# Eight blocks of the first feed-forward computed for both token halves at once, each pair of weight blocks in seven block products instead of eight

## The chip, the cores and the metric

The kernel runs on one core of a Trainium2 chip. A core has a matrix engine (TensorE, PE in the profile, with its weight loads as PEld), a vector engine (VectorE, DVE), a scalar engine (ScalarE, ACT), a general engine (GpSimd, POOL) and a queue that issues transfers (SyncE, SP). Each engine takes its instructions strictly in the order in which the program lists them; semaphores make one wait for another. The metric is device time in microseconds (us), lower is better.

## What is computed

The reference is a two-layer trunk on 1024 tokens with 1024 channels, in float32. Layer 0 mixes tokens by a forgetting attention and a pooling mixer, layer 1 by an RWKV-7 recurrence, and each is followed by a gated feed-forward of width 2816:

```python
def _swiglu(h, w_gate, w_up, w_down):
    return (jax.nn.silu(h @ w_gate) * (h @ w_up)) @ w_down

for layer in range(DEPTH):                 # DEPTH = 2
    h = _rmsnorm(x, mix_norm[layer])
    y = fox_pool_mixer(h) if layer == 0 else rwkv7_time_mix(h)
    x = x + y
    x = x + _swiglu(_rmsnorm(x, ffn_norm[layer]), ffn_w_gate[layer], ffn_w_up[layer], ffn_w_down[layer])
```

The change concerns the feed-forward of layer 0.

## The kernel before

Activations lie transposed: channels on the 128 partitions, tokens along the free axis. The tokens are split in two halves of 512, so a half of an activation is 8 tiles of 128x512, one per 128 channels. Every float32 operand is split into a rounded high part and a remainder (`part`, lines 257 to 261, for activations: a ScalarE copy, line 259, and a VectorE subtraction, line 260; `load_part`, lines 140 to 153, for weights: a transfer, line 150, a copy, line 151, a subtraction, line 152), and one product of a 128x128 weight block with a 128x512 activation is three matmuls (`mm3`, lines 163 to 165).

The feed-forward (`ffn`, from line 683) goes through 22 blocks of 128 hidden columns. A block of one token half is 24 matmuls for the gate, 24 for the up projection, and later 24 for its share of the down projection: 72 matmuls. Its VectorE work is the remainders of six 128x512 weight tiles, the gating products (lines 726 and 732), the remainder of the result (line 260) and two of the eight additions into the residual (line 705).

The program runs the two token halves one after the other, because the first half has to reach the recurrence early:

- Half 0 of the first feed-forward runs by itself: four blocks (`GP`), then eighteen (`G1`), in groups of four and a last group of two. The matrix engine has nothing else to do in this stretch.
- `rw.dense(0, ...)` computes the projections of the recurrence for half 0.
- The recurrence of half 0 is two jobs, `rw.job(0, 0)` and `rw.job(1, 0)`, of eight heads each. A job has a **preparation** (lines 1007 to 1148: scans, decay factors, small matmuls at lines 1029, 1060, 1074 and 1085, the inverse of triangular blocks as a chain of VectorE steps at lines 1096 to 1120, and four groups of 64 tiny matmuls at lines 1130 and 1140, each followed by copies, line 121 on ScalarE and line 123 on VectorE) and a **chunk loop** (lines 1157 to 1192: eight dependent chunks, each a chain of small matmuls at lines 1165, 1171, 1177, 1188 and 1190 with copies between, lines 1167, 1173, 1179, 1183).
- Half 1 of the first feed-forward is a generator, `f1`, that serves as **filler**: its 22 blocks (1584 matmuls, named `fm` in the profile) are handed out between the steps of the two jobs. `weave` takes as many matmuls from the filler as the main stream yields, and the jobs yield what `rw.fr` says: seven numbers per token half, one for each kind of step. 96 matmuls of `f1` are issued ahead of the projections, what is left after the jobs is issued by `run(f1)`, and then the same things follow for half 1, with layer 1's feed-forward as filler.

A scheduler orders each engine's instructions when the program is built, by the order in which they were written and by when their operands should be ready; on the chip the order is fixed. Tile pools decide how many buffers each kind of tile has: five for split weights (`k.wbufs`), two for raw ones (`k.rawbufs`), four PSUM tiles for products (`k.mm`) in this stretch.

The norm ahead of the feed-forward of half 1 is `on[1]`: eight squares and sums, a matmul with a constant (line 307), a logarithm and an exponential (lines 309, 310, each with a table load on ScalarE here), then `make_h` (lines 675 to 680) scales the eight tiles and splits them. Before, this stands behind the four blocks of `GP`.

Of the kernel before, what the change touches and what calls it, by code (L numbers as in the profile page):

```python
# [9 lines left out]
F32 = mybir.dt.float32  # L10
F32R = mybir.dt.float32r
AF = mybir.ActivationFunctionType
ALU = mybir.AluOpType
# [3 lines left out]
P = 128  # L17
# [3 lines left out]
HN = 512  # L21
FF = 2816
NFB = FF // P
# [57 lines left out]
def rd(ap):  # L81
    return ap.bitcast(F32)
# [53 lines left out]
def load_w(k, ap, tag="w", w=512, bufs=None, pool=None):  # L136

    p, n = ap.shape
    return [load_part(k, ap[:, c:c + min(512, n)], p, min(512, n), tag, w, bufs, pool) for c in range(0, n, 512)]


def load_part(k, ap, p, n, tag="w", w=512, bufs=None, pool=None):
    hi, lo = ((pool or k.wp).tile([P, w], F32R, tag=tag + i, name=nm(k, tag + i), bufs=bufs or k.wbufs) for i in ("hi", "lo"))
    raw = k.wp.tile([P, 512], F32, tag="wraw", name=nm(k, "wraw"), bufs=k.rawbufs)
    dst = raw[0:p, 0:n]
    if len(ap.shape) == 3:
        dst = dst.rearrange("p (a b) -> p a b", b=ap.shape[2])
# [4 lines left out]
    k.nc.vector.tensor_tensor(lo[0:p, 0:n], raw[0:p, 0:n], rd(hi[0:p, 0:n]), ALU.subtract)  # L152
    return hi, lo


def mm3(k, out, pairs, first=True, last=True):

    nc = k.nc  # L160
    n = len(pairs)
    for i, ((wh, wl), (xh, xl)) in enumerate(pairs):
        nc.tensor.matmul(out, wh, xh, start=(first and i == 0), stop=False)  # L163
        nc.tensor.matmul(out, wh, xl, start=False, stop=False)  # L164
        nc.tensor.matmul(out, wl, xh, start=False, stop=(last and i == n - 1))  # L165
        yield 3


# [42 lines left out]
def ahead(fill, n):  # L211

    while n > 0:
        n -= next(fill)
# [41 lines left out]

def part(k, hl, raw):
    hi, lo = hl
    k.nc.scalar.copy(hi, raw)  # L259
    k.nc.vector.tensor_tensor(lo, raw, rd(hi), ALU.subtract)  # L260
    return hi, lo
# [412 lines left out]
def make_h(k, norm, gain, x, acc, out, rs=None):  # L674
    nc = k.nc
    rs = rs or norm.rstd()
    for kt in range(KT):
        t = norm.tile("hn")
        nc.vector.scalar_tensor_tensor(t, x[kt], cvec(k, gain, kt), rs, ALU.mult, ALU.mult)
        out[kt] = part(k, pair(k, *acc), t)  # L680


def ffn(k, ins, L, halves, H, X, acc, tp, groups, after=None, silu=True, fb0=0):
    nc = k.nc

    def project(w):
        o = {half: pmm(k) for half in halves}
        for c in range(2):
            for half in halves:
                yield from mm3(k, o[half], [(blk(w, kt), H[half][kt]) for kt in range(4 * c, 4 * c + 4)], c == 0, c == 1)  # L690
        return o

    def down(n, fb0, acts, last):
        per = max(1, 4 // n)
        cur = None
        for half, m in [(half, m) for half in halves for m in range(8)] if last else [(half, m) for m in range(8) for half in halves]:
            if cur != m // per:
                cur = m // per
                w = []
                for f in range(0, n, 4):  # L700
                    c = min(4, n - f)
                    w.append(load_part(k, ins[f"wd{L}"][per * cur:per * cur + per, :, fb0 + f:fb0 + f + c].rearrange("m p f c -> p m f c"), P, per * c * P))
            o = pmm(k)
            yield from mm3(k, o, [(blk(w, (m % per) * n + i), acts[fb0 + i, half]) for i in range(n)])
            nc.vector.tensor_tensor(X[half][m], o, X[half][m], ALU.add)  # L705
            if last:
                after(half, m)


    behind = iter(())  # L710
    for gi, n in enumerate(groups):
        acts, sgs = {}, {}
        for fb in range(fb0, fb0 + n):
            g = yield from project(load_w(k, ins[f"wg{L}"][fb]))
            for half in halves:
                sg = sgs[half] = tp.tile([P, HN], F32, tag="nt", name=nm(k, "sg"), bufs=k.ntbufs)
                if silu:
                    k.last_silu = nc.scalar.activation(sg, g[half], AF.Silu)
                elif silu is None and k.sigm:
                    k.last_sig = nc.scalar.activation(sg, g[half], AF.Sigmoid)  # L720
                    nc.vector.tensor_tensor(sg, g[half], sg, ALU.mult)
                else:
                    nc.scalar.activation(sg, g[half], AF.Exp, scale=-1.0)
                    nc.scalar.activation(sg, sg, AF.Ln, bias=1.0)
                    nc.scalar.activation(sg, sg, AF.Exp, scale=-1.0)
                    nc.vector.tensor_tensor(sg, g[half], sg, ALU.mult)  # L726
# [9 lines left out]
    yield from behind  # L736


EXP_M05 = 0.6065306597126334
# [496 lines left out]
def build(ctx, tc, ins, outs, dbg=None, stop=99):  # L1236
    nc = tc.nc
    k = K()
# [5 lines left out]
    H = [[None] * KT for _ in range(2)]  # L1244
    X = [[None] * KT for _ in range(2)]
    xT = ins["xT"]
    outT = outs["out"]
    rw = Rwkv(k, ins, dram)

    def pool(n, side="left"):  # L1250
        c = ExitStack()
        p = c.enter_context(tc.tile_pool(name=n, bufs=1, side=side, reuse_waits="tile"))
        return c, p

    def psum(n):
        c = ExitStack()
        p = c.enter_context(tc.tile_pool(name=n, bufs=1, space=PSUM))
        return c, p
# [11 lines left out]
    c_x0, x0 = pool("x0")  # L1270
# [7 lines left out]
    y, sp = {}, {}  # L1278
# [27 lines left out]
    c_m, mp = pool("m1", "right")  # L1306
    c_t, tp = pool("t1", "right")
# [13 lines left out]
    on = [Norm(k, tp) for _ in range(2)]  # L1321
# [13 lines left out]
    c_wl, wl = pool("wl")  # L1335
    c_u, u = pool("u")
    U, M = (u, "u", 40), (mp, "h1", 24)
    make_h(k, on[0], "ffn0", X[0], U, H[0], rs0)
    c_ps.close()
    c_pf, pf = psum("psf")  # L1340
    c_ps, k.ps = psum("ps1")
    k.mm = (k.ps, "mm", 4)

    norms = [Norm(k, tp), Norm(k, mp)]

# [9 lines left out]
            cover[half]()  # L1355
            rw.norm(half, norms[half].rstd(), XT[half])

    GP, G0, G1, G2 = ((4,),(),(4,4,4,4,2),(4,4,4,4,2))
    n = sum(GP) + sum(G0)
    g0 = ffn(k, ins, 0, (0,), H, X, U, tp, GP)  # L1360
# [5 lines left out]
    run(ffn(k, ins, 0, (0, 1), H, X, U, tp, G0, fb0=sum(GP)))  # L1366
    run(ffn(k, ins, 0, (0,), H, X, U, tp, G1, after0, True, n))
    rw.ln_exp, rw.mx, rw.wl_bufs, k.sigm = False, U, 2, True
    f1 = chain(ffn(k, ins, 0, (1,), H, X, M, mp, GP, silu=None), ffn(k, ins, 0, (1,), H, X, M, mp, G2, after0, None, n))
# [4 lines left out]
    for c in (c_u, c_wl, c_x0, c_t, c_ps):  # L1374
        c.close()
    c_ps, k.ps = psum("ps2")
    k.sbufs = 3
# [43 lines left out]
    c_t, tp = pool("tail0")  # L1421
# [129 lines left out]
```

## Time and profile before

| | |
|---|---|
| runs (3) | 2702.07 us median, 2700.6 to 2703.24 |
| the profiled execution's own time | 2699.79 us |
| its span | 2698.0 us |
| PE busy | 2632.5 us, 98% of the span, 15368 matmuls |
| DVE busy | 1725.1 us, 64%, 2940 instructions |
| ACT busy | 1298.7 us, 48%, 2297 instructions |
| chain of work that ended last | PE 77%, DVE 14%, ACT 3%, DMA 3%, issue 3% |

How to read it: the span is what the profiler saw between the first and the last instruction, 1.79 us less than the execution's own time. PE's busy time counts matmuls from start to end, and they overlap, so PE can read as 100% busy and still be held back for a moment. A row of a table of windows gives, for a stretch of the span in us, the stretch's length and then each engine's busy time with the number of instructions, the granted TensorE clock as a share of full speed, the share of time that the DMA engines moved data, and GB/s. A row of a timeline is the start, the duration, the engine, the line, the operation, the tiles written and read, and in brackets how long the engine sat idle before it and what ended that.

### The profile page before, as it was taken

How to read it: one execution, taken by the hardware profiler on the slowest of the kernel's cores; microseconds unless marked ns; L12 is line 12 of the kernel's file. 1: busy time of each engine (PE TensorE's matmuls, PEld its weight loads, DVE VectorE, ACT ScalarE, POOL GpSimd, SP SyncE). 2: the span in 40 equal slices, each digit the busy share in tenths (PEclk: the TensorE clock that was granted, in tenths of full speed). 3: DMA queues.
4: the chain of work that ended last, by engine and by line, in shares of the span. 5: the costliest groups of instructions: out<-in, count | busy, mean ns of one | idle time of the engine just before them, and what ended most of it. 6: DMA issues, size and time to landing. Idle time of an engine off the chain costs nothing.

```text
span 2698.0 us, 40269 instructions
## 1 busy us (share of the span) xinstructions
PE 2632.5 (98%) x15368; PEld 2072.6 (77%) x15368; DVE 1725.1 (64%) x2940; ACT 1298.7 (48%) x2297; POOL 49.4 (2%) x139
## 2 busy tenths in 40 slices
PE   8999999999999999999999999999999999999999
PEld 6787878788888777777777677777777777888887
DVE  8777684653446655975995676469778856534443
ACT  7555564443224766434634467664445444332232
POOL 1000000000001000000000000000000000000000
PEclk9999999999999999999999999999999999999999
DMA  4111131233333545424433534554244336333333
GB/s 136 58 51 57 42 98 48 83 96 98 96 96 113 172 161 189 129 83 131 148 91 99 195 94 160 168 179 128 87 138 140 92 97 202 101 98 96 97 97 94
DMA packets 170529, 306.11 MB, mean 113 GB/s; under 512 B 18896, under 2 KB 26192, under 8 KB 170336
## 3 DMA queue, kind: packets, MB, share of 16 engines
q1 hardware_dynamic: 156512, 278.38, 33.5%
q10 hardware_dynamic: 13824, 25.17, 2.5%
q8 instruction: 120, 1.97, 0.3%
q14 instruction: 73, 0.60, 0.1%
HBM read 257.04 MB, written 46.43 MB: 112 GB/s over the span
## 4 chain that ended last, share of the span: by engine, by line
PE 77%; DVE 14%; ACT 3%; DMA 3%; issue 3%; SPq 0%; DVEq 0%; ACTq 0%
PE mm L163 16%; PE mm L164 16%; PE mm L165 16%; PE fm L163 6%; PE fm L164 5%; PE fm L165 5%; DVE wlo L152 2%; PE mm L175 1%; DVE nu L1112 1%; DVE pd L1110 1%; DVE ZL L1068 1%; DMA wraw<-in_wd_dram 1%; DMA wraw<-in_wu_dram 1%; ACT whi L151 1%; PE o L1177 1%
## 5 line engine op out<-in xcount | busy, mean ns | idle before, releaser
L151 ACT CAST whi<-wraw 128x512 fp32r<-128x512 f32 x738 | 454.0, 617 | 886.8 <-PE mm L164 484.5
L152 DVE TENSOR_TENSOR wlo<-wraw,whi 128x512 fp32r<-128x512 f32 x738 | 501.3, 683 | 446.0 <-ACT whi L151 436.4
L163 PE MATMUL mm<-hh,whi 128*128 128x512 f32 x864 | 343.7, 400 | 6.7 <-ACT hh L355 6.2
L165 PE MATMUL mm<-hh,wlo 128*128 128x512 f32 x864 | 338.7, 392 | 0.0
L164 PE MATMUL mm<-hl,whi 128*128 128x512 f32 x864 | 337.8, 392 | 0.0
L163 PE MATMUL mm<-uh,whi 128*128 128x512 f32 x728 | 283.5, 391 | 0.9 <-DVE x L1318 0.9
L165 PE MATMUL mm<-uh,wlo 128*128 128x512 f32 x728 | 283.1, 389 | 1.2 <-DVE wlo L152 1.2
L164 PE MATMUL mm<-ul,whi 128*128 128x512 f32 x728 | 283.2, 390 | 0.0
L163 PE MATMUL fm<-h1h,whi 128*128 128x512 f32 x528 | 218.7, 415 | 14.8 <-DVE sg L726 10.6
L165 PE MATMUL fm<-h1h,wlo 128*128 128x512 f32 x528 | 208.7, 396 | 0.5 <-DVE wlo L152 0.5
L164 PE MATMUL fm<-h1l,whi 128*128 128x512 f32 x528 | 208.5, 395 | 0.1
L163 PEld LDWEIGHTS mm<-hh,whi 128*128 128x128 f32 x864 | 162.5, 188 | 43.1 <-ACT hh L355 6.9
L165 PEld LDWEIGHTS mm<-hh,wlo 128*128 128x128 f32 x864 | 162.7, 188 | 34.8 <-DVE wlo L152 0.6
L164 PEld LDWEIGHTS mm<-hl,whi 128*128 128x128 f32 x864 | 162.9, 189 | 32.7 <-DVE hl L260 1.3
L163 PE MATMUL fm<-hh,whi 128*128 128x512 f32 x416 | 172.4, 414 | 3.5 <-ACT hh L259 2.8
L164 PE MATMUL fm<-hl,whi 128*128 128x512 f32 x416 | 164.5, 396 | 0.2 <-DVE hl L260 0.2
L165 PE MATMUL fm<-hh,wlo 128*128 128x512 f32 x416 | 164.6, 396 | 0.0
L163 PEld LDWEIGHTS mm<-uh,whi 128*128 128x128 f32 x728 | 136.5, 188 | 34.6 <-issue 2.7
L164 PEld LDWEIGHTS mm<-ul,whi 128*128 128x128 f32 x728 | 136.6, 188 | 31.1 <-issue 1.1
L165 PEld LDWEIGHTS mm<-uh,wlo 128*128 128x128 f32 x728 | 136.7, 188 | 30.0 <-DVE wlo L152 2.0
L705 DVE TENSOR_TENSOR x<-mm,x 128x512 f32<-128x512 f32 x96 | 66.2, 692 | 119.8 <-PE mm L165 119.6
L163 PEld LDWEIGHTS fm<-h1h,whi 128*128 128x128 f32 x528 | 99.5, 189 | 48.7 <-DVE sg L726 13.3
(338 smaller groups left out, 4632.4 us busy)
## 6 DMA issues: line engine op xcount, KB each, us to landing
wraw<-in_wg_dram SPq DMA_DIRECT2D x176, 256.0 KB, 2.8
wraw<-in_wu_dram SPq DMA_DIRECT2D x176, 256.0 KB, 2.7
wraw<-in_wd_dram SPq DMA_DIRECT2D x176, 256.0 KB, 2.7
wraw<-in_w_in_dram SPq DMA_DIRECT2D x52, 256.0 KB, 2.9
x<-in_xT_dram SPq DMA_DIRECT2D x32, 256.0 KB, 4.8
x<-x SPq DMA_DIRECT2D x32, 256.0 KB, 3.1
wraw<-in_w_k_dram SPq DMA_DIRECT2D x32, 256.0 KB, 2.9
wraw<-in_w_v_dram SPq DMA_DIRECT2D x32, 256.0 KB, 3.0
```

Of the source, the lines that this page charges most:

```text
L151: k.nc.scalar.copy(hi[0:p, 0:n], raw[0:p, 0:n])
L152: k.nc.vector.tensor_tensor(lo[0:p, 0:n], raw[0:p, 0:n], rd(hi[0:p, 0:n]), ALU.subtract)
L163: nc.tensor.matmul(out, wh, xh, start=(first and i == 0), stop=False)
L164: nc.tensor.matmul(out, wh, xl, start=False, stop=False)
L165: nc.tensor.matmul(out, wl, xh, start=False, stop=(last and i == n - 1))
L175: k.nc.tensor.matmul(out[n * q:n * q + n], w[:, n * j:n * j + n], xs[j], start=c == 0, stop=c + g == len(xs), tile_position=(0, n * q))
L705: nc.vector.tensor_tensor(X[half][m], o, X[half][m], ALU.add)
L1068: nc.vector.tensor_tensor(ZL[h][HS[1 - h], i, bs], s4[HS[1]], self.msk[HS[1]].rearrange("p a t -> p (a t)").unsqueeze(1).broadcast_to([64, ...
L1110: nc.vector.tensor_tensor(pv, nu[:, j + 1:32, j:j + 1].broadcast_to([P, n, j]), nu[:, j:j + 1, 0:j].broadcast_to([P, n, j]), ALU.mult)
L1112: nc.vector.tensor_tensor(nu[:, j + 1:32, 0:j], nu[:, j + 1:32, 0:j], pv, ALU.add)
L1177: nc.tensor.matmul(sp[HS[h], i], BK[h][:, i, c], uv[h][:, i], start=True, stop=True)
```

## The change

For eight of the 22 blocks of layer 0's feed-forward, four pairs, gate and up are computed for both token halves together. A pair of weight blocks is a 2x2 arrangement (two halves of the channels by two blocks), the normed activations another (two halves of the tokens by two halves of the channels), and their product is done by Strassen's scheme in Winograd's form: seven products of 12 matmuls instead of eight, on sums and differences of the operands. `Joint.rows` builds the sums of the activations once, `Joint.four` builds those of the weights, runs the seven products and adds up their results, `Joint.down` does the down projection of a pair for both halves. Half 0's own run falls from 18 blocks behind `GP` to 10, and the filler `f1` from 22 to 14. `rw.fr` for half 0 is lowered, the products get six PSUM tiles instead of four, and the pool `wl` opens after the joint part, on the other side of the memory. Line numbers from 739 on are 148 higher in the changed kernel.

```diff
-def mm3(k, out, pairs, first=True, last=True):
+def mm3(k, out, pairs, first=True, last=True, again=False):
...
+class Joint:
...
+    def rows(self, gain, rs, H, U, M, keep):
...
+        for j in range(4):
+            a22 = normed(self.mt("a22"), 1, j + 4)
+            H[1][j + 4] = part(k, pair(k, *M), a22)
+            A["22"].append(H[1][j + 4])
+            a21 = normed(self.n3("a21"), 1, j)
+            nc.sync.dma_start(keep(j), a21)
+            s1 = self.nt("s1")
+            nc.vector.tensor_tensor(s1, a21, a22, ALU.add)
+            A["S1"].append(part(k, pair(k, *U), s1))
+            a11 = normed(self.jt("a11", "tt", 3), 0, j)
+            s2 = self.nt("s2")
+            nc.vector.tensor_tensor(s2, s1, a11, ALU.subtract)
+            A["S2"].append(part(k, pair(k, *U), s2))
+            nc.vector.tensor_tensor(a11, a11, a21, ALU.subtract)
+            A["S3"].append(part(k, pair(k, *M), a11))
+            a12 = normed(self.jt("a12", "tc", 2), 0, j + 4)
+            nc.vector.tensor_tensor(a12, a12, s2, ALU.subtract)
+            A["S4"].append(part(k, pair(k, *U), a12))
+            yield 0
...
+    def four(self, w, f, out):
...
+        p11 = self.split(b11)
+        t3, t2, t4 = (self.jt(n, "tt", 3) for n in ("t3", "t2", "t4"))
+        nc.vector.tensor_tensor(t3, b22, b12, ALU.subtract)
+        nc.vector.tensor_tensor(b12, b12, b11, ALU.subtract)
+        nc.vector.tensor_tensor(t2, b22, b12, ALU.subtract)
+        pt2 = self.split(t2)
+        x = pmm(k)
+        yield from product(x, p11, "11")
+        s1 = self.n3("p1")
+        nc.scalar.copy(s1, x)
+        p21 = self.split(b21)
+        nc.vector.tensor_tensor(t4, b21, t2, ALU.subtract)
+        y = pmm(k)
+        yield from product(y, pt2, "S2")
+        u = self.n3("u")
+        nc.vector.tensor_tensor(u, y, s1, ALU.add)
+        pt1 = self.split(b12)
+        yield from product(x, p21, "12", False)
+        out(0, 0, x, None)
...
+        yield from product(v, pt4, "22", False)
+        out(1, 0, v, u)
...
-    k.mm = (k.ps, "mm", 4)
+    k.mm = (k.ps, "mm", 6)
...
-    GP, G0, G1, G2 = ((4,),(),(4,4,4,4,2),(4,4,4,4,2))
...
+    GP, NJ = (4,), 4
+    left = NFB - sum(GP) - 2 * NJ
+    G1 = tuple(min(4, left - i) for i in range(0, left, 4))
+    fj, n = sum(GP), sum(GP) + 2 * NJ
+    g0 = ffn(k, ins, 0, (0,), H, X, M, tp, GP)
     ahead(g0, 24)
     for m in MO[1][NP:]:
         on[1].add(X[1][m])
-    run(g0)
-    make_h(k, on[1], "ffn0", X[1], M, H[1])
...
+    ahead(g0, 48)
+    jn = Joint(k, ins, 0, X, tp, mp, jp, M)
+    for _ in jn.rows("ffn0", (rs0, on[1].rstd()), H, U, M, lambda j: rw.dt(f"n{j}")):
+        ahead(g0, 24)
+    run(jn.run(fj, NJ, g0))
...
-    rw.fr = [6, 6, 5, 16, 7, 9, 16], [7, 7, 4, 16, 7, 8, 20]
+    rw.fr = [4, 4, 3, 8, 3, 9, 8], [7, 7, 4, 16, 7, 8, 20]
```

The order changes at two places that matter below. On VectorE, behind the sums of squares of half 1's norm, there stood only what the next blocks of half 0 need: remainders of weights (`wlo`), the gating product (`sg`) and the remainder of its result (`ul`).

```order
L732 TENSOR_TENSOR sg_4881<-mm_4895,sg_4881 128x512
L152 TENSOR_TENSOR wlo_4965<-wraw_4966,whi_4964 128x512
L152 TENSOR_TENSOR wlo_4971<-wraw_4972,whi_4970 128x512
L260 TENSOR_TENSOR ul_4922<-sg_4881,uh_4921 128x512
L152 TENSOR_TENSOR wlo_5007<-wraw_5008,whi_5006 128x512
```

At the same place of the changed kernel stand the rows of `Joint.rows` (lines 775 to 794, and 260 for their remainders). This is the end of the third of its four rounds; `wlo_5159` and `wlo_5165` are the weights of the next product of half 0, which TensorE runs before it comes to the joint part.

```order
L775 SCALAR_TENSOR_TENSOR a_1282_5149<-x_4538,cv,rs_4713 128x512
L789 TENSOR_TENSOR s_1277_5138<-s_1273_5130,a_1276_5136 128x512
L260 TENSOR_TENSOR ul_5133<-s_1273_5130,uh_5132 128x512
L791 TENSOR_TENSOR a_1276_5136<-a_1276_5136,a_1272_5126 128x512
L260 TENSOR_TENSOR ul_5141<-s_1277_5138,uh_5140 128x512
L794 TENSOR_TENSOR a_1282_5149<-a_1282_5149,s_1277_5138 128x512
L260 TENSOR_TENSOR h1l_5146<-a_1276_5136,h1h_5145 128x512
L152 TENSOR_TENSOR wlo_5159<-wraw_5160,whi_5158 128x512
L260 TENSOR_TENSOR ul_5153<-a_1282_5149,uh_5152 128x512
L152 TENSOR_TENSOR wlo_5165<-wraw_5166,whi_5164 128x512
```

So `wlo_5159` has moved behind 35 VectorE instructions that need half 1's norm, the first of them being the scaling of a tile by `rs_4964`; the next product's weights (`wlo_5237`) stand 17 rows further on.

On TensorE, near the end of the first job's preparation, filler matmuls (`fm`) stood between the groups of tiny matmuls (lines 1130 and 1140), of which these are the last two.

```order
L163 MATMUL fm_10826<-h1h_10293,whi_10820 128x512
L164 MATMUL fm_10826<-h1l_10294,whi_10820 128x512
L165 MATMUL fm_10826<-h1h_10293,wlo_10821 128x512
L163 MATMUL fm_10826<-h1h_10407,whi_10820 128x512
L164 MATMUL fm_10826<-h1l_10408,whi_10820 128x512
L165 MATMUL fm_10826<-h1h_10407,wlo_10821 128x512
L1140 MATMUL s_10833<-XR_9420,g_10796 32x32 x32
```

In the changed kernel (lines 1278 and 1288 are 1130 and 1140) nearly all of the filler of this part has gone.

```order
L1278 MATMUL s_11406<-t_2655_11375,XR_10428 32x32 x32
L165 MATMUL fm_11727<-h1h_7337,wlo_11716 128x512
L163 MATMUL fm_11727<-h1h_7343,whi_11715 128x512
L164 MATMUL fm_11727<-h1l_7344,whi_11715 128x512
L165 MATMUL fm_11727<-h1h_7343,wlo_11716 128x512
L1288 MATMUL s_11448<-XR_10428,g_11439 32x32
L1278 MATMUL s_11492<-t_2655_11375,XR_10428 32x32 x32
```

Counted in these orders, TensorE gets 403 filler matmuls in the first job's preparation before and 249 after, 432 and 269 in the second's; 168 and 76 in the first chunk loop, 168 and 72 in the second; 57 and 43 between the first loop and the second preparation. VectorE has 214 instructions in the first preparation before and 186 after, 224 and 191 in the second; of each number 144 or 146 are the job's own.

More of the change, by code (lines that the diff above doesn't have):

```diff
@@ L162, in mm3 @@
     for i, ((wh, wl), (xh, xl)) in enumerate(pairs):
-        nc.tensor.matmul(out, wh, xh, start=(first and i == 0), stop=False)
-        nc.tensor.matmul(out, wh, xl, start=False, stop=False)
-        nc.tensor.matmul(out, wl, xh, start=False, stop=(last and i == n - 1))
+        nc.tensor.matmul(out, wh, xh, start=(first and i == 0), stop=False, skip_group_check=again)
+        nc.tensor.matmul(out, wh, xl, start=False, stop=False, skip_group_check=again)
+        nc.tensor.matmul(out, wl, xh, start=False, stop=(last and i == n - 1), skip_group_check=again)
         yield 3
@@ L1334, in build @@
     c_h.close()
-    c_wl, wl = pool("wl")
     c_u, u = pool("u")
+    c_j, jp = pool("joint", "right")
     U, M = (u, "u", 40), (mp, "h1", 24)
@@ L1356, in after0 @@
             rw.norm(half, norms[half].rstd(), XT[half])
-    GP, G0, G1, G2 = ((4,),(),(4,4,4,4,2),(4,4,4,4,2))
-    n = sum(GP) + sum(G0)
-    g0 = ffn(k, ins, 0, (0,), H, X, U, tp, GP)
+    GP, NJ = (4,), 4
[3 more added lines that the diff above has]
+    g0 = ffn(k, ins, 0, (0,), H, X, M, tp, GP)
     ahead(g0, 24)
@@ L1363, in build @@
         on[1].add(X[1][m])
-    run(g0)
-    make_h(k, on[1], "ffn0", X[1], M, H[1])
-    run(ffn(k, ins, 0, (0, 1), H, X, U, tp, G0, fb0=sum(GP)))
+    ahead(g0, 48)
[3 more added lines that the diff above has]
+    run(jn.run(fj, NJ, g0))
+    for j in range(4):
+        t = jn.n3("a21")
+        nc.sync.dma_start(t, rw.dt(f"n{j}"))
+        H[1][j] = part(k, pair(k, *M), t)
+    c_j.close()
+    c_wl, wl = pool("wl", "right")
     run(ffn(k, ins, 0, (0,), H, X, U, tp, G1, after0, True, n))
     rw.ln_exp, rw.mx, rw.wl_bufs, k.sigm = False, U, 2, True
-    f1 = chain(ffn(k, ins, 0, (1,), H, X, M, mp, GP, silu=None), ffn(k, ins, 0, (1,), H, X, M, mp, G2, after0, None, n))
+    f1 = chain(ffn(k, ins, 0, (1,), H, X, M, mp, GP, silu=None), ffn(k, ins, 0, (1,), H, X, M, mp, G1, after0, None, n))
     f1 = using(k, f1, mm=(pf, "fm", 2), ntbufs=3)
@@ L1373, in build @@
     weave(rw.dense(0, XT[0], wl, tp), (f1, share))
-    for c in (c_u, c_wl, c_x0, c_t, c_ps):
+    for c in (c_u, c_x0, c_wl, c_t, c_ps):
         c.close()
```

74 lines of the change are left out of this document (added).

## The prediction

> **What bounds the kernel now.** The page first: TensorE is busy nearly all the time, so an idle engine elsewhere is worth nothing, and the question is how fast matmuls follow each other and where they don't. The table of windows answers both.
>
> ```profile
> span 2698.0 us, 40269 instructions
> ...
> PE 2632.5 (98%) x15368; PEld 2072.6 (77%) x15368; DVE 1725.1 (64%) x2940; ACT 1298.7 (48%) x2297; POOL 49.4 (2%) x139
> ...
> core 0: us, PE busy (x) PEld busy (x) DVE busy (x) ACT busy (x) POOL busy (x), PEclk, DMA share, GB/s
> ...
> 600.00:700.00 100.00, 100.00 (x443) 82.81 (x442) 41.66 (x63) 28.62 (x47) 0.00 (x0) 1.00 0.33 98
> 1050.00:1187.00 137.00, 126.83 (x970) 98.54 (x969) 125.28 (x212) 71.64 (x129) 4.44 (x15) 0.99 0.40 125
> 1187.00:1258.00 71.00, 71.00 (x855) 54.36 (x851) 38.29 (x73) 28.73 (x61) 0.25 (x1) 1.00 0.32 101
> 1258.00:1267.00 9.00, 9.00 (x43) 5.30 (x38) 2.94 (x6) 6.26 (x11) 0.74 (x2) 1.00 0.21 60
> 1267.00:1405.00 138.00, 129.73 (x852) 99.72 (x852) 131.56 (x222) 68.55 (x122) 4.20 (x16) 0.99 0.43 133
> 1405.00:1477.00 72.00, 72.00 (x923) 55.48 (x916) 39.39 (x72) 34.14 (x69) 0.00 (x0) 1.00 0.33 99
> 1477.00:1520.00 43.00, 41.34 (x236) 28.87 (x232) 27.25 (x46) 16.27 (x30) 0.00 (x0) 1.00 0.50 161
> ```
>
> 600 to 700 us is half 0's feed-forward alone: 443 matmuls in 100 us, 0.2257 us from one to the next, and VectorE 42% busy. This stretch is bound by TensorE and nothing else. 1050 to 1477 us are the two jobs of half 0: preparation, chunk loop, a short end, preparation, chunk loop. In the preparations **VectorE is busy 91% and 95%** (125.28 of 137, 131.56 of 138) and TensorE 93% and 94%: two engines are full at once. In the chunk loops TensorE is full and VectorE at 54%. So a matmul taken from the first stretch or from a chunk loop is worth its 0.2257 us; one taken from a preparation is worth only what VectorE loses with it. The list of waits confirms who is late there: its longest row for TensorE in the first preparation is a wait for VectorE.
>
> ```profile
> PE fm L163 <- DVE sg L726: 5.7, 3, 4.1
> ```
>
> **The change part by part.** *Matmuls.* Each gate or up of a pair takes 84 matmuls instead of 96; eight of them save 96, in all 96 x 0.2257 = 21.7 us. The mean duration of a matmul is no measure of that:
>
> ```profile
> L165 PE MATMUL mm<-uh,wlo 128*128 128x512 f32 x728 | 283.1, 389 | 1.2 <-DVE wlo L152 1.2
> ```
>
> 389 ns each would make it 37.3 us, but they overlap. The Trainium skill ("TensorE: Matmul & The Clock Gate", section "Wait — 56ns, not 53.3ns?") gives 215.7 ns from start to start at 512 columns; by it the saving would be an estimated 20.7 us. The trace's 225.7 ns decides.
>
> The 96 are a difference of two large moves. Half 0's run goes from 18 blocks (18 x 72 = 1296 matmuls) to four pairs of 264 and ten blocks of 72 (1776): 480 more, +108.3 us, all in a stretch where TensorE is alone. The filler loses eight blocks, 576 matmuls, 130.0 us. The orders show from where: 154 from the first preparation, 163 from the second, 188 from the chunk loops, 14 between, and the other 57 after the jobs.
>
> *Preparations.* 154 and 163 matmuls are 34.8 and 36.8 us of TensorE. VectorE loses 28 and 33 instructions, nearly all of 128x512. One of those costs this much in a row of them:
>
> ```profile
> 498.70 0.69 DVE L302 TENSOR_TENSOR sq<-sq,sq 128x512 f32<-128x512 f32 x1
> 499.30 0.68 DVE L260 TENSOR_TENSOR ul<-hn,uh 128x512 fp32r<-128x512 f32 x1
> 499.90 0.69 DVE L302 TENSOR_TENSOR sq<-sq,sq 128x512 f32<-128x512 f32 x1
> ```
>
> 0.60 us from start to start. So the preparations get shorter by 28 x 0.60 = 16.8 and 33 x 0.60 = 19.8 us, and 18.0 + 17.0 = 35.0 us of the matmuls taken out turn into idle TensorE. After the change TensorE's own work in the first preparation is 126.83 - 403 x 0.2257 = 36 us plus 249 x 0.2257 = 56 us, 92 us, against a VectorE floor of 125.28 - 16.8 = 108.5 us: the cover is gone, and VectorE alone is late. Bounds: if VectorE gets to 100% busy, the preparations last 108.5 and 131.56 - 19.8 = 111.8 us, and 16.9 us are lost; if the copies between the tiny matmuls, which have lost their filler, add 3 us to each, 41. I take 35, since VectorE's share was 91 to 95% with the filler there.
>
> *Chunk loops.* Here is a chunk without its filler: the matmuls of line 1165, the copy that waits for them, line 1171, its copies, then line 1177 and its two steps.
>
> ```profile
> 1191.06 0.69 PE L1165 MATMUL s<-SV,ZL 128*64 128x64 f32 x16
> ...
> 1191.79 0.42 DVE L1167 COPY zs<-s 128x256 f32<-128x256 f32 x1 [1.37 <-PE s L1165]
> ...
> 1193.26 0.68 PE L1171 MATMUL s<-zs,XR 64*64 64x64 f32 x16
> ...
> 1193.99 0.76 ACT L1173 COPY uv<-s 64x256 f32<-64x256 f32 x2 [0.93 <-PE s L1171]
> ...
> 1213.32 0.69 PE L1177 MATMUL o<-uv,BK 128*64 128x64 f32 x16
> ...
> 1214.05 0.42 DVE L1179 TENSOR_TENSOR st<-o,S 128x256 f32<-128x256 f32 x1 [0.71 <-PE o L1177]
> ...
> 1214.51 0.87 DVE L1183 TENSOR_TENSOR SV<-st,Pc 64x256 f32<-64x256 f32 x2
> ```
>
> From line 1165 to its copy's end 1.15 us, from line 1171 to its copies' end 1.49, from line 1177 to the new state 2.06: 4.7 us a chunk if nothing is in the way. A chunk lasts 71 / 8 = 8.9 us now and loses 92 / 8 = 11.5 matmuls, 2.6 us, to 6.3. The chain still fits, with 1.6 us to spare, but three matmuls (0.7 us) behind line 1171 no longer cover its copies, and a 0.6 us split ahead on ScalarE or VectorE then stalls TensorE. I take 0.4 us a chunk, 16 chunks, 6 us; bounds 2 and 14 (nothing but the bare chain; a split ahead at half of the three hand-overs).
>
> *Entry to the joint part.* `Joint.rows` adds 13 VectorE instructions in each of four rounds and needs half 1's norm. The norm comes after 72 matmuls that begin here:
>
> ```profile
> 492.62 0.70 PE L163 MATMUL mm<-uh,whi 128*128 128x512 f32 x2 [0.88 <-DVE x L1318]
> ```
>
> so at 492.6 + 72 x 0.2257 = 508.9 us. From that matmul to the first scaled tile the same norm took, later in the kernel before,
>
> ```profile
> 558.42 1.02 PE L307 MATMUL mm<-sq,cc 128*128 128x512 f32 x2
> ...
> 562.98 2.08 DVE L679 SCALAR_TENSOR_TENSOR hn<-x,cv,rs 128x512 f32<-128x512 f32 x3 [3.08 <-ACT rs L310]
> ```
>
> 4.6 us, with both table loads; one more split on ScalarE makes it 5.1. So the rows begin at about 514.0, and `wlo_5159`, 35 instructions behind the first, is ready at 514.0 + 36 x 0.61 = 536.0 (0.60, and a little more for the scalings, 0.66 us apart by the row above). TensorE has two products of 24 that need none of it, to 508.9 + 1.0 + 48 x 0.2257 = 520.7, and then waits about 15 us. The 24 end at 541.4; `wlo_5237` comes 17 rows later, at 546.4, another 5 us. After that the joint products' own weights are ready in time. Together **20 us**. In the kernel before, the norm waited behind `GP` and cost TensorE nothing. Bounds: 17 (0.55 us an instruction, 8% closer than these rows) and 24 (0.3 for each of ten waits on ScalarE besides). What hides none of this is VectorE's later slack: its order is fixed.
>
> *Inside the joint part* a pair is 264 matmuls, 59.6 us; VectorE has some 60 instructions for it, 37 us, and the order puts each product's weights at least one product (2.7 us) ahead. I take 3 us for the one place where products of `down` follow the last of `four` directly (add, product, split: about 2.7 us by these durations); bounds 0 and 12 (0.2 us at each of 56 products). Fewer weight transfers and splits are under TensorE anyway: nothing. The 57 + 14 matmuls elsewhere lie in windows with TensorE full: counted in the 21.7.
>
> **Sum:** -21.7 + 35.0 + 6 + 20 + 3 = +42.3 us. Against the profiled execution's own 2699.79 that is 2742; the median of the runs shown is 2.3 us above that execution (0.08%), well inside the bounds. Low ends together -21.7 + 16.9 + 2 + 17 + 0 = +14 (2714), high ends -21.7 + 41 + 14 + 24 + 12 = +69 (2769).
>
> **Rivals.** *VectorE is not the bound (faster).* If its instructions could stand closer, both the idle preparations and the entry's wait would go: 2699.8 - 21.7 + 9 = 2687. It would decide if 186 instructions fitted under TensorE's 92 us, 0.49 us each. For it speaks only that TensorE is as full as VectorE now; against it, that the mean of a busy preparation is 131.56 / 222 = 0.59 us with 5% idle. *A cold TensorE (slower still).* The preparations' rows grant a clock of 0.99 where the longest wait is 4.1 us, and 1.00 elsewhere. Waits of 15 us at the entry and repeated ones in the preparations could run their small matmuls, some 36 us in each, partly at a lower clock; a third of them at half speed is 12 us each on the way to VectorE: 2766. The Trainium skill ("TensorE: Matmul & The Clock Gate", section "What's actually happening") says that one idle window of about 3.4 us halves the clock until about 3.4 us of work have passed; the 0.99 agrees in sign. *Joint products stall at each hand-over (slower still).* A sum that arrives late at each of 56 products by 0.6 us is 34 us: 2773. Against it: five split buffers, and the products' weights stand ahead of the additions in the order. *The change doesn't save matmuls:* excluded by the orders, which hold 96 fewer.
>
> **How the numbers follow.** Forecast with its bounds, 2714 to 2769: 74%. VectorE not the bound: 7%. Both stalls at half, about 2706: 4%. Cold TensorE: 8%, half of it inside the forecast's bounds. Joint stalls: 7%. For the range I leave out the first rival and most of the last: 2707 to 2772. A difference of 0.2% is what a measurement of this kernel can tell from none; below 2696.7 lies most of the first rival, 6%; between that and 2707.5 5%; above 89%.
>
> **What would show it.** Right: a TensorE wait of 10 us or more for a `wlo` of line 152 around 520 us; preparations of 115 to 123 us with VectorE over 88% busy and TensorE under 82%; chunk loops of 52 to 56 us; half 0's feed-forward about 130 us later at its end. Wrong: preparations near 100 us, or no long wait at the entry. The sum fails if the chunk loops lose their cover altogether, or if the joint products wait for their sums.

## The result, and the profile after

The changed kernel takes **2736.42 us** (median of 4 runs, 2734.26 to 2741.7) against 2702.6 us (4 runs, 2700.6 to 2703.24): ratio **1.0129, 95% interval 1.0112 to 1.0147**, slower by 34 us. Its profiled execution took 2734.26 us. The page of the changed kernel begins:

```profile
span 2732.5 us, 40037 instructions
...
PE 2636.0 (96%) x15272; PEld 2075.3 (76%) x15272; DVE 1791.5 (66%) x3052; ACT 1287.5 (47%) x2281; POOL 50.2 (2%) x139
```

There are 96 matmuls fewer, and yet TensorE is busy 3.5 us longer: some matmuls have become slower. The table of windows shows where. The first row of each kernel runs from the start of the norm's 72 matmuls (492.6 us) to the first scan of the first job; then come preparation, chunk loop (first to last copy `zs`), the stretch between the jobs, preparation, chunk loop, and all the rest. Before:

```profile
492.60:1051.18 558.58, 557.38 (x2435) 449.67 (x2436) 286.19 (x441) 260.09 (x435) 11.73 (x22) 1.00 0.40 124
1051.18:1191.79 140.61, 130.44 (x1016) 101.35 (x1015) 126.77 (x215) 72.19 (x129) 4.44 (x15) 0.99 0.39 121
1191.79:1252.54 60.75, 60.75 (x717) 46.39 (x718) 33.06 (x64) 25.02 (x55) 0.00 (x0) 1.00 0.32 100
1252.54:1275.25 22.71, 22.71 (x140) 14.58 (x139) 13.11 (x23) 11.77 (x21) 1.11 (x3) 1.00 0.41 126
1275.25:1420.14 144.89, 136.62 (x1047) 106.79 (x1046) 133.73 (x225) 72.05 (x128) 4.09 (x15) 0.99 0.41 126
1420.14:1480.56 60.42, 60.42 (x716) 46.00 (x717) 32.16 (x63) 28.01 (x59) 0.00 (x0) 1.00 0.32 98
1480.56:2698.00 1217.44, 1186.10 (x7065) 928.78 (x7065) 746.95 (x1211) 547.18 (x959) 11.36 (x38) 0.99 0.40 126
```

After:

```profile
492.60:1182.27 689.67, 670.57 (x2919) 542.47 (x2920) 412.56 (x642) 298.13 (x499) 12.15 (x22) 0.99 0.33 104
1182.27:1298.05 115.78, 102.35 (x861) 79.81 (x860) 108.56 (x186) 56.63 (x104) 3.95 (x15) 0.88 0.36 115
1298.05:1342.79 44.74, 44.74 (x632) 32.55 (x631) 26.98 (x55) 21.20 (x48) 0.00 (x0) 0.96 0.36 113
1342.79:1364.64 21.85, 21.31 (x131) 12.81 (x131) 12.23 (x22) 9.81 (x18) 1.18 (x3) 1.00 0.29 83
1364.64:1484.44 119.80, 105.06 (x875) 80.92 (x876) 111.86 (x193) 58.98 (x106) 4.17 (x15) 0.92 0.39 120
1484.44:1527.11 42.67, 42.67 (x626) 30.86 (x624) 26.78 (x55) 17.96 (x43) 0.00 (x0) 0.99 0.37 119
1527.11:2732.50 1205.39, 1171.33 (x6996) 916.99 (x6996) 739.24 (x1200) 542.09 (x950) 12.10 (x38) 0.99 0.40 125
```

What a stage lost is its change in time, less 0.2257 us for each matmul more or fewer in it (the counts in brackets behind PE):

| stage | time before, after (us) | matmuls, at 0.2257 | lost |
|---|---|---|---|
| to the first scan | 558.58, 689.67 | +484: +109.2 | 21.9 |
| preparation 1 | 140.61, 115.78 | -155: -35.0 | 10.2 |
| chunk loop 1 | 60.75, 44.74 | -85: -19.2 | 3.2 |
| between | 22.71, 21.85 | -9: -2.0 | 1.2 |
| preparation 2 | 144.89, 119.80 | -172: -38.8 | 13.7 |
| chunk loop 2 | 60.42, 42.67 | -90: -20.3 | 2.6 |
| the rest | 1217.44, 1205.39 | -69: -15.6 | 3.5 |
| sum | +34.5 | -96: -21.7 | 56.3 |

So 56 us were lost against 21.7 saved. The first loss stands in the list of TensorE's waits (what waits, for whom, us in all, times, longest) as one row, and in the timeline as two matmuls:

```profile
PE mm L165 <- DVE wlo L152: 17.4, 2, 15.4
...
537.62 0.80 PE L165 MATMUL mm<-uh,wlo 128*128 128x512 f32 x1 [15.44 <-DVE wlo L152]
538.22 0.63 PE L163 MATMUL mm<-uh,whi 128*128 128x512 f32 x1
538.64 0.63 PE L164 MATMUL mm<-ul,whi 128*128 128x512 f32 x1
...
548.10 0.50 PE L165 MATMUL mm<-uh,wlo 128*128 128x512 f32 x1 [1.97 <-DVE wlo L152]
```

The two waits are `wlo_5159` and `wlo_5237` of the order. Between them stand 24 matmuls that take 548.10 - 537.62 - 1.97 = 8.5 us instead of 24 x 0.2257 = 5.4: behind the long wait they are 0.43 us apart. Entry: 15.4 + 2.0 + 3.1 = 20.5 us. Those 3.1 us cost nothing of their own: the second weights come when VectorE has made them, and faster matmuls would only have waited longer for them. From 600 to 1100 us TensorE is 99.8% busy, and of the stage's 21.9 us only 1.4 are left for everything but the entry; so the joint products hardly stall.

### The profile page after: what moved, and what is told of

Its sections match the earlier page's. It is cut to its first block, busy times and chain, and to the rows that moved or that the text cites. A ratio compares the mean times of both kernels' runs of the same rounds, so it can differ in the third digit from the quotient of the medians.

```text
span 2732.5 us, 40037 instructions
## 1 busy us (share of the span) xinstructions
PE 2636.0 (96%) x15272; PEld 2075.3 (76%) x15272; DVE 1791.5 (66%) x3052; ACT 1287.5 (47%) x2281; POOL 50.2 (2%) x139
## 3 DMA queue, kind: packets, MB, share of 16 engines
q8 instruction: 120, 1.97, 0.3%
## 4 chain that ended last, share of the span: by engine, by line
PE 75%; DVE 14%; DMA 4%; ACT 4%; issue 2%; SPq 0%; ACTq 0%; DVEq 0%
PE mm L163 17%; PE mm L164 17%; PE mm L165 17%; PE fm L163 5%; PE fm L165 4%; PE fm L164 4%; DVE wlo L152 2%; PE mm L175 1%; DVE ZL L1216 1%; PE s L1313 1%; ACT whi L151 1%; DMA wraw<-in_wg_dram 1%; PE o L1325 1%; DVE nu L1260 1%; PE s L1319 1%
## 5 line engine op out<-in xcount | busy, mean ns | idle before, releaser
L151 ACT CAST whi<-wraw 128x512 fp32r<-128x512 f32 x658 | 404.3, 616 | 774.8 <-PE mm L164 444.3
L152 DVE TENSOR_TENSOR wlo<-wraw,whi 128x512 fp32r<-128x512 f32 x658 | 446.9, 683 | 389.6 <-ACT whi L151 382.2
L165 PE MATMUL mm<-uh,wlo 128*128 128x512 f32 x664 | 259.6, 392 | 17.5 <-DVE wlo L152 17.4
L163 PE MATMUL mm<-uh,whi 128*128 128x512 f32 x664 | 259.6, 393 | 1.2 <-DVE x L1466 1.2
L164 PE MATMUL mm<-ul,whi 128*128 128x512 f32 x664 | 259.1, 391 | 0.0
L165 PEld LDWEIGHTS mm<-uh,wlo 128*128 128x128 f32 x664 | 125.3, 189 | 44.6 <-DVE wlo L152 18.8
L163 PE MATMUL fm<-h1h,whi 128*128 128x512 f32 x336 | 141.4, 421 | 8.5 <-DVE x L705 5.9
L165 PE MATMUL fm<-h1h,wlo 128*128 128x512 f32 x336 | 140.3, 418 | 1.4 <-DVE wlo L152 1.4
L164 PE MATMUL fm<-h1l,whi 128*128 128x512 f32 x336 | 139.0, 414 | 0.1
L163 PEld LDWEIGHTS fm<-hh,whi 128*128 128x128 f32 x416 | 79.1, 190 | 31.1 <-issue 8.1
```

The source lines that it names most:

```text
L164: nc.tensor.matmul(out, wh, xl, start=False, stop=False, skip_group_check=again)
```

## The experiments

**Is it the filler?** *The kernel before, with the changed `rw.fr`, without the joint part.*

```diff
-    rw.fr = [6, 6, 5, 16, 7, 9, 16], [7, 7, 4, 16, 7, 8, 20]
+    rw.fr = [4, 4, 3, 8, 3, 9, 8], [7, 7, 4, 16, 7, 8, 20]
```

> The kernel before with nothing changed but the seven numbers of rw.fr for half 0, which are set as in the changed kernel: the two jobs get the thin filler, the rest of the filler is issued after them; no joint part. Theory A (the loss of the two jobs comes from taking filler out of them, as the stages of the two traces add up: preparations 23.2 us, chunk loops 7.1, the stretch between and the one after 2.9): 2702.6 + 33 = 2736 us, between 2730 and 2742. By the prices of the prediction (35 + 6) it would be 2744. Rival B (the loss belongs to the joint part, its memory or its clock): 2703 us.

2740.01 us, ratio 1.0141 (1.0128 to 1.0154): 38 us lost with not one matmul fewer. By the same reckoning preparation 1 loses 10.6 us (10.2 in the changed kernel), preparation 2 16.2, the loops 3.3 and 3.7. The losses of the jobs need no joint part; rival B falls. (The time stands between theory A's 2736 and the 2744 by the prediction's prices.)

*Only the preparations' six numbers lowered* (`[4, 4, 3, 8, 7, 9, 8]`):

> The kernel before with rw.fr of half 0 lowered only for the preparations (six of the seven numbers, the fifth stays 7). Theory A: 23 to 24 us of loss, 2727 us (2721 to 2732), each preparation some 25 us shorter but with some 155 to 170 matmuls fewer. By the prediction's price 2738. Rival B (TensorE alone bounds the preparations, so that filler goes in and out at its own price): 2703 us.

*Only the chunk loops' number lowered* (`[6, 6, 5, 16, 3, 9, 16]`):

> The kernel before with rw.fr of half 0 lowered only for the chunk loops (the fifth number 7 becomes 3). Theory A (the chain of a chunk is no longer covered at some hand-overs): 7 us of loss, 2710 us (2707 to 2714), chunks of some 6.1 to 6.4 us instead of 8.6. Rival B (the loops stay bound by TensorE): 2703 us.

2718.13 us, 1.0067 (1.0055 to 1.0079), and 2712.98 us, 1.0038 (1.0025 to 1.0052). The first run is a miss: it cost less than theory A said, although the scheduler took 75 matmuls out of its loops too; its two preparations lost 9.1 and 7.7 us. The second run came out in its range but lost its time elsewhere than expected: its loops got shorter by 18.2 and 19.1 us for 84 matmuls (19.0) each, so they lost under 1 us together, while preparation 2 and the rest, whose numbers were not touched, lost 5.5 each, which stays open. Nor do the two add up to the first run: 1.05% against 1.41%. By the stages of the profiled executions, 3 us of the difference lie in preparation 2 (with the loops left full it kept more of its filler, 916 matmuls against 871), 3 in chunk loop 2 and 2 behind the jobs.

**Is it VectorE?** The prediction called VectorE full in the preparations. *The filler's weights that are loaded during the jobs get no remainder* (the third matmul of a product takes the rounded weights once more), in both kernels:

```diff
     k.nc.scalar.copy(hi[0:p, 0:n], raw[0:p, 0:n])
+    if getattr(k, "nolo", False):
+        return hi, hi
```

> The changed kernel, in which the filler's weights that are loaded during the two jobs of half 0 get no remainder (load_part returns the rounded part twice): 20 and 23 VectorE subtractions fewer in the two preparations, 7 or 8 fewer in each chunk loop, the same matmuls. Theory A (VectorE's count of instructions sets the length of the thinned preparations): 20 x 0.60 = 12.0 and 23 x 0.60 = 13.8 us shorter at most, preparations of 103 to 107 us instead of 116 and 120, 2736.4 - 24 = 2712 us (2704 to 2718). Rival B (the job's own chain through ScalarE, VectorE and TensorE sets it): preparations within 4 us of the changed kernel's, 2728 us or more.

> The kernel before with the same edit: 36 and 39 VectorE subtractions fewer in the two preparations, the same matmuls. Theory A (before the change VectorE and TensorE are both full there, so VectorE relieved by more than 20 us leaves TensorE as the bound): each preparation 8 to 10 us shorter, near 131 and 137 us, 2702 - 17 = 2685 us (2680 to 2691). Rival B (the preparation's idle TensorE comes from the job's own chain): 2697 us or more.

Before: 2700.05 us, 1.0004 (0.9995 to 1.0013). Nothing, where theory A wanted 17 us. The two preparations of that run:

```profile
1053.72:1191.34 137.62, 129.72 (x1014) 102.42 (x1013) 107.28 (x179) 71.03 (x128) 4.04 (x15) 0.98 0.38 123
...
1275.88:1422.28 146.40, 136.26 (x1043) 107.01 (x1042) 110.69 (x185) 71.10 (x128) 4.14 (x15) 0.98 0.39 124
```

VectorE falls from 90 and 92% to 78 and 76%, the lengths hardly move. So in the kernel before, VectorE's load does not set the length of a preparation. TensorE is busy for 93 and 94% of it, and the 8 to 10 us in which it is idle stay when VectorE is relieved; what makes them, this run does not show. Theory A falls for that kernel. After: 2720.6 us, 1.0077 (1.0063 to 1.0091), 16 us less than the changed kernel, not 24; the preparations last 106.0 and 115.2 us instead of 115.8 and 119.8. The matmuls were not quite the same: the preparations hold 21 and 7 fewer. Beyond these they got 5.0 and 3.0 us shorter with 17 and 20 VectorE instructions fewer. There VectorE's load does count, but less than 0.60 us for each instruction. The chunk loops gained too: they lose 0.3 and 0.6 us instead of 3.2 and 2.6.

**Which part of the preparation?** So I cut the preparations of both kernels into stretches. The scaling and the products (lines 1012 to 1090 before), and the four groups of tiny matmuls up to the chunk loop, in the first job before:

```profile
1062.78:1117.60 54.82, 50.79 (x410) 39.08 (x410) 53.10 (x86) 29.52 (x57) 2.83 (x5) 1.00 0.47 149
...
1158.43:1191.79 33.36, 29.30 (x369) 23.01 (x368) 24.43 (x27) 12.55 (x21) 0.00 (x0) 0.95 0.25 73
```

and after:

```profile
1193.41:1241.47 48.06, 38.68 (x344) 30.66 (x344) 45.86 (x75) 25.74 (x52) 2.34 (x5) 0.86 0.45 143
1241.47:1282.47 41.00, 39.49 (x197) 31.03 (x195) 39.22 (x90) 17.50 (x31) 0.75 (x6) 1.00 0.33 98
1282.47:1298.05 15.58, 13.56 (x282) 10.95 (x283) 13.10 (x10) 3.98 (x7) 0.00 (x0) 0.56 0.05 16
```

The scaling loses 66 matmuls (14.9 us) and gets 6.8 us shorter: VectorE, 95% busy, is late, as predicted, and 8.1 us are lost. TensorE's longest waits in it are for VectorE:

```profile
PE s L1208 <- DVE ZL L1216: 3.5, 3, 1.4
PE o L1222 <- DVE bk L1192: 3.3, 1, 3.3
```

The groups lose 87 matmuls (19.6 us) and get 17.8 us shorter: VectorE was 73% busy there, so TensorE gave back nearly the whole price. With the filler gone the first group now waits for VectorE's transposition (line 1268), and the groups' tiny matmuls run slow from there on:

```profile
1284.49 1.91 PE L1278 MATMUL s<-t,XR 32*32 32x32 f32 x64 [2.98 <-DVE t L1268]
```

The inverse between the two (the middle row of after) keeps its filler and its length. In the second job the scaling (before, then after) loses 10.6 us for 74 matmuls, with VectorE at 91% after, and the groups (the last two rows) 3.7 for 96.

```profile
1287.38:1347.08 59.70, 56.38 (x438) 43.55 (x438) 56.64 (x92) 36.67 (x67) 2.91 (x6) 1.00 0.51 159
```

```profile
1375.22:1428.79 53.57, 45.94 (x364) 35.27 (x364) 48.99 (x79) 27.61 (x53) 3.00 (x6) 0.87 0.43 134
```

```profile
1388.69:1420.14 31.45, 31.32 (x381) 24.92 (x380) 25.83 (x29) 9.57 (x16) 0.00 (x0) 0.98 0.25 74
```

```profile
1470.98:1484.44 13.46, 10.01 (x285) 7.63 (x286) 13.18 (x12) 4.68 (x8) 0.00 (x0) 0.92 0.01 2
```

That VectorE is the late one in the thinned scaling, the changed kernel without remainders bears out. These are its two scaling stretches:

```profile
1195.19:1239.57 44.38, 37.48 (x349) 29.90 (x349) 43.24 (x70) 27.98 (x55) 2.69 (x5) 0.92 0.48 155
...
1365.79:1418.06 52.27, 47.52 (x411) 38.90 (x412) 46.34 (x74) 29.61 (x57) 3.49 (x6) 0.92 0.43 144
```

In each, five VectorE instructions are gone. The first is 3.7 us shorter with five matmuls more; the second took 47 matmuls more (10.6 us) and still got 1.3 us shorter, so TensorE had room there.

Two runs of the kernel before try it, with filler taken from the groups alone, `[6, 6, 5, 8, 7, 9, 16]`, and from the first two stretches alone, `[4, 4, 5, 16, 7, 9, 8]`:

> The kernel before with one number of rw.fr for half 0 lowered, the fourth (16 becomes 8): filler is taken from between the four groups of tiny matmuls at the end of each preparation, and from nowhere else; it is issued after the jobs. Theory S (a preparation is several stretches with different limits; the stretch of the groups was TensorE's, so it gets shorter by nearly the price of the matmuls): the stretch falls from 33.4 and 31.5 us to some 15 and 14, about 5 us are lost, 2707 us (2703 to 2712). Theory F (the flat price of the prediction, VectorE late over the whole preparation: 35 us for 317 matmuls, 0.11 us each): some 180 matmuls cost 20 us, 2721 us.

> The kernel before with the first, second and seventh number of rw.fr for half 0 lowered (6, 6, 16 become 4, 4, 8): filler is taken only from the first two stretches of each preparation, the scans, the scaling and the products of lines 1009 to 1085, some 155 matmuls in both jobs together. Theory S (there VectorE becomes the one that is late, 91 to 95% busy in the changed kernel, and the matmuls taken out save less than half their time): 18 to 22 us are lost, 2721 us (2716 to 2727). Theory F (0.11 us each): 17 us, 2718 us; it and the run without the groups' filler must lose alike by F, and four times as much here by S.

The groups: 2701.37 us, 1.0002 (0.9993 to 1.0011). The scheduler took only some 70 matmuls from the two preparations, not 180, since it refilled part of the gap; at the flat price of 0.11 us they would still have cost 7.7 us, and over the whole run they cost nothing that can be measured, less even than the 5 us that theory S expected. The groups of its two jobs:

```profile
1159.38:1185.81 26.43, 23.20 (x339) 17.78 (x339) 20.70 (x22) 10.97 (x19) 0.00 (x0) 0.94 0.24 70
...
1391.03:1415.75 24.72, 21.23 (x324) 16.09 (x323) 20.89 (x22) 7.38 (x13) 0.00 (x0) 0.86 0.18 59
```

In the first job they are 6.9 us shorter for 30 matmuls (6.8 us), as theory S has it. In the second they are 6.7 us shorter for 57 (12.9 us), and that preparation as a whole loses 8.7 us, which the profiled execution gained back behind the jobs (6.1 us). Why is open. The scaling: 2713.53 us, 1.0050 (1.0037 to 1.0062), 13 us for 148 matmuls out of the two preparations, less than the 18 to 22 expected but plainly a loss. Its scaling stretch in the first job is the changed kernel's over again, without any of the change:

```profile
1063.16:1111.29 48.13, 38.82 (x346) 31.10 (x346) 46.43 (x75) 26.33 (x53) 2.41 (x5) 0.86 0.46 148
```

In the second job it is not: 40 matmuls are gone there, and only 0.9 us are lost.

```profile
1281.51:1333.08 51.57, 45.12 (x398) 35.31 (x400) 49.70 (x81) 33.48 (x64) 3.15 (x6) 0.93 0.48 150
```

So theory S holds for the two runs as wholes and for the first job: what a filler matmul is worth hangs on the stretch from which it is taken. A price for each stretch that holds in both jobs, these runs do not give.

**The entry.** *The rounds of `Joint.rows` 72 matmuls apart, among eight blocks of half 0.* Its later rounds read tiles of X to which the first four blocks' down projection has already been added, so it computes something other than the reference; it serves to find the cause and is no version to use.

```diff
-    GP, NJ = (4,), 4
+    GP, NJ = (4, 4), 4
...
-        ahead(g0, 24)
+        ahead(g0, 72)
```

> The changed kernel with the four rounds of Joint.rows 72 matmuls apart instead of 24, and eight blocks of half 0 instead of four for them to stand in (GP = (4, 4)); four pairs as before. Theory A (the entry costs 17.4 us of waits and 3 us of a lower clock behind them): the first wlo needed behind the rows now has 2 instructions ahead of it that need the norm and the next ones 15 to 29, so that one wait of 3 to 4 us is left, and the clock stays up; 2736.4 - 17 = 2719 us (2715 to 2724). Rival B (the rows' work is only pushed on, and the wait comes back for the first weights of the joint part): 2733 to 2737 us.

2715.51 us, 1.0054 (1.0039 to 1.0070), 21 us less than the changed kernel. The list of waits has, up to the first scan:

```profile
PE mm L165 <- DVE wlo L152: 3.0, 3, 2.3
```

and that stage loses 8.0 us instead of 21.9 (675.85 against 558.58 us, 484 matmuls more); 3.0 of the 8.0 are these waits. The long wait does not come back. *In half rounds, 21 matmuls apart, among the four blocks:*

```diff
             A["S1"].append(part(k, pair(k, *U), s1))
+            yield 0
...
-        ahead(g0, 24)
+        ahead(g0, 21)
```

> The changed kernel with each round of Joint.rows cut in two (a second yield behind the split of s1) and 21 matmuls of half 0 between the eight half rounds, GP = (4,) as in the change: everything that the reference asks for is computed. The first wlo that TensorE lacks has 16 instructions that need the norm or stand behind one ahead of it, instead of 35. Theory A (the entry's loss is the wait for VectorE's rows and the clock behind it): a wait of some 4 us instead of 17.4, no slow stretch behind it, 2736.4 - 15 = 2721 us (2716 to 2725). Rival B: the wait returns at the next weights, 2733 us or more.

2732.12 us, 1.0120 (1.0102 to 1.0138): only 4 us better than the change. The wait came back, in pieces, as rival B had it:

```profile
PE mm L165 <- DVE wlo L152: 8.2, 4, 3.8
...
510.00:520.00 10.00, 10.00 (x44) 7.99 (x43) 6.33 (x11) 8.67 (x12) 0.00 (x0) 1.00 0.25 88
520.00:530.00 10.00, 6.18 (x22) 4.64 (x21) 10.00 (x17) 5.45 (x10) 0.00 (x0) 0.85 0.23 79
530.00:540.00 10.00, 8.47 (x37) 6.63 (x36) 7.35 (x13) 3.56 (x7) 0.00 (x0) 0.98 0.32 102
540.00:550.00 10.00, 9.59 (x41) 7.11 (x40) 10.00 (x18) 6.29 (x12) 0.00 (x0) 1.00 0.45 138
550.00:560.00 10.00, 7.36 (x29) 5.47 (x28) 9.96 (x18) 3.00 (x5) 0.00 (x0) 0.89 0.29 85
```

VectorE is full from 520 to 530 and from 540 to 560 us. The 52 instructions of the rows are 31 us of VectorE; in 168 matmuls, 38 us, half 0's own blocks at 42% need another 16. The expectation looked at the first weights that TensorE lacks and not at this sum. With 72 matmuls between the rounds there are 65 us for it, and it fits.

**Towards a better mix.** *Two pairs, half rounds, filler taken from the chunk loops and from behind the jobs* (`NJ = 2`, `[6, 6, 5, 16, 4, 9, 16]`), and *four pairs, half rounds, the filler of the scaling put back* (`[6, 6, 3, 8, 3, 9, 16]`):

> Two pairs instead of four (NJ = 2: 48 matmuls saved, 288 of filler gone), the rows in half rounds as above, and the filler taken out of the chunk loops (fifth number 7 becomes 4) and of the stretch behind the jobs, not out of the preparations. Theory A (a loss hangs on where filler is missing; the preparations are where it costs most): -10.8 for the matmuls, 5 to 6 at the entry, 1 to 5 in the loops, 2 to 3 behind: 2701 us (2695 to 2707). Rival B (a matmul of filler costs the same wherever it is missing, 33 us for 576, so 16 for 288): 2713 us.

> The changed kernel with the rows in half rounds (as in the run of that name, 2732 us) and with rw.fr for half 0 at [6, 6, 3, 8, 3, 9, 16]: the filler of the first two stretches of the preparations is as before the change, taken from what the changed kernel had left over behind the jobs. Theory S: the 18 to 21 us of the first two stretches come back, and up to 7 us are lost behind the jobs, where two pairs instead of four lost that for 153 matmuls: 2716 us (2710 to 2722), still slower than before by some 15. Rival (filler is worth the same behind the jobs as in front): 2728 us or more.

Two pairs: 2718.94 us, 1.0074 (1.0060 to 1.0089), a miss. The loops lost nothing for 127 matmuls (0.5 us gained), but the entry cost 13.7 us where I had put 6, the stretch behind the jobs 7.7 for 153 matmuls, and the preparations 8 us with their filler untouched, which I can't explain. Four pairs with the scaling's filler: 2715.86 us, 1.0057 (1.0044 to 1.0071), where 2716 was expected. Against the run with half rounds alone that is 16 us for a mere move of filler: the scaling is 53.95 us long with 407 matmuls (54.82 with 410 before the change), and the stretch behind the jobs loses 6.5 us (225 matmuls fewer, 44.2 us shorter). No version here beats the kernel before. The stages of this last run say why: against the 21.7 us that four pairs save stand 13.6 at the entry, 9.6 still in the preparations (1.6 and 8.1), 5.9 in the loops, 1.8 between the jobs and 6.5 behind them. Even with the 8.0 us entry of the run with 72 matmuls between the rounds it would be an estimated 10 us slower than the kernel before.

## Why the prediction was right, and where not

**Matmuls, -21.7 us: right.** The counts differ by 96, and a matmul in the joint part costs what it costs elsewhere (600 to 700 us: 443 in 100 us in both kernels).

**Entry, +20, and inside the joint part, +3: right.** Together 21.9 us measured against 23. The first scaled tile comes at 515.4 us (514.0 forecast), the two weights are ready at 537.6 and 548.1 (536.0 and 546.4), the wait is 15.4 (15). The second wait was 2.0 us instead of 5, because the matmuls ahead of it ran 3.1 us longer at a low clock, which the sum did not have; together they are the 5 us, since VectorE sets when the second weights come. That the long wait is for the rows, the run with 72 matmuls between them shows; why VectorE is full there, the run in half rounds.

**Preparations, +35: mis-sized; 23.9 us.** The step that failed is "the preparations get shorter by 28 x 0.60 = 16.8 and 33 x 0.60 = 19.8 us". They got shorter by 24.8 and 25.1. It took VectorE's 91 and 95% of a whole preparation for the limit of each of its parts. The groups' stretch of the first job had VectorE at 73%; there TensorE was the limit, and more than half of the first preparation's matmuls came from there, at 0.02 us lost each (1.8 / 87) against 0.12 in the scaling (8.1 / 66). In the second job it is 0.04 (3.7 / 96) against 0.14 (10.6 / 74). The premise "two engines are full at once" did not hold as it was used either: relieving VectorE by some 20 us in each preparation of the kernel before did nothing. In the changed one VectorE is late in the scaling, as the prediction said, at 95 and 91%. TensorE under 82% was wrong: it reads 88% in both, and the granted clock is 0.88 and 0.92, so its matmuls take longer.

**Chunk loops, +6: right in size (5.8) by luck, not in reason.** The prediction laid it to copies no longer covered. The run with loops thinned alone lost 0.6 us in the two. In the changed kernel the first loop's first chunk is the long one, 8.81 us at a clock of 0.82, the next 6.76 at 1.00:

```profile
1298.05:1306.86 8.81, 8.81 (x96) 6.24 (x95) 5.81 (x11) 4.17 (x10) 0.00 (x0) 0.82 0.40 121
1306.86:1313.62 6.76, 6.76 (x93) 4.86 (x94) 5.72 (x12) 4.08 (x10) 0.00 (x0) 1.00 0.70 233
```

The low clock of the groups' stretch, 0.56, reaches into it. With its preparation full and the loop equally thin, the first chunk took 6.55 us for 94 matmuls; the difference, 2.3 us, is most of that loop's 3.2. In the second loop the first chunk lasts 7.02 us at 0.92, and most of the 2.6 us there stays open.

**What the sum left out:** 4.7 us between and behind the jobs, counted as nothing. The 3.5 behind the jobs are no sure loss: in the kernel before without remainders the same stretch, with the same matmuls, came out 4.5 us shorter. The sum came to +42.3, the spans differ by 34.5: 11 us too many for the preparations and 1 for the entry, less these. That the total came so near owes something to two errors of opposite sign.

**The rivals.** *VectorE not the bound*: true of the preparations of the kernel before, where relieving it gained nothing; not of the changed kernel, where VectorE is late at the entry and in the scaling. *A cold TensorE*: true in part. The clock is 0.88 and 0.92 in the preparations, and a group of 64 tiny matmuls takes 1.92 us where it took 1.20:

```profile
1291.78 1.92 PE L1288 MATMUL s<-XR,g 32*32 32x32 f32 x64
```

```profile
1186.31 1.20 PE L1140 MATMUL s<-XR,g 32*32 32x32 f32 x64
```

(the first of the changed kernel, the second of the one before). By the rows of the stages, TensorE is idle for only 3.3 and 6.5 us longer in the two preparations; the other 14 of the 23.9 us are matmuls that follow each other more slowly. That does not make the clock the cause of 14 us: where VectorE is late, faster matmuls would have waited longer, as at the entry. What each would cost without the other was not separated. *Joint products stall*: no.

## What to carry to other kernels

Work that fills gaps has no single price. Before it is taken away, cut the stretch that it fills where the limit changes, and read for each part which engine is the other full one: in the changed kernel the same filler matmul cost 0.02 to 0.04 us in one stretch and 0.12 to 0.14 in another. Then test it by itself: here the prices of the first job did not all return in the second. Where a scheme saves matmuls by additions on another engine, look first at the place where those additions come all at once, and set their sum, with the work already there, against the time that the matmuls issued meanwhile give.

## What the hardware showed besides

The granted clock fell after shorter waits than I had reckoned with. In the run with half rounds a wait of 3.82 us is followed by four matmuls at full rate and then eight 0.43 us apart, and one of 2.47 us by 13 at once:

```profile
558.65 0.79 PE L165 MATMUL mm<-h1h,wlo 128*128 128x512 f32 x1 [2.47 <-DVE wlo L152]
559.24 0.63 PE L163 MATMUL mm<-h1h,whi 128*128 128x512 f32 x1
559.67 0.63 PE L164 MATMUL mm<-h1l,whi 128*128 128x512 f32 x1
```

Waits of 1.53 us (in that run) and 1.97 us (in the changed kernel) were followed by matmuls at full rate. So a wait of 2.5 us may cost 13 x 0.2 = 2.6 us more, unless a later wait takes them up as at the entry. The Trainium skill ("TensorE: Matmul & The Clock Gate", section "What's actually happening") speaks of an idle window of about 3.4 us that runs freely. The 15.4 us wait agrees, with 13 slow matmuls over 5.7 us behind it; the 2.47 us one is shorter than that window.
